# Two of four weight sums made by adding transfers instead of VectorE

## The chip, the cores and the metric

The kernel runs on one core of one Trainium2 chip. The metric is the time of one execution on the device in microseconds (us), lower is better. All arrays are float32. A core has five engines that work side by side, each with its own instructions in a fixed order: TensorE (matrix products; PE in the profile, PEld for its weight loads), VectorE (DVE), ScalarE (ACT), GpSimd (POOL) and SyncE (SP), which here only issues transfers. Transfers between the main memory (HBM) and the on-chip memory (SBUF) run on 16 DMA engines.

## The reference

One layer of a hybrid block works on 256 rows of 4096 numbers. What matters here are its large matrix products; the attention and the convolution between them are left out of this cut:

```python
xn = rms_norm(h, norm_in_g[i])
proj = xn @ w_in[i]                       # q, k, v, z_a, a_c, g_c, z_c: 14336 columns
...
y_a = rms_norm(y_a, attn_out_g[i]) * jax.nn.silu(z_a)
...
y_c = rms_norm(y_c, conv_out_g[i]) * jax.nn.silu(z_c)
h = h + jnp.concatenate([y_a, y_c], axis=-1) @ w_out[i]
gate = jax.nn.sigmoid(rms_norm(h, ple_norm_g[i]) @ w_ple_gate[i] + b_ple_gate[i])
h = h + gate * (p[i] @ w_ple[i])
```

## The kernel before, in words

All large products are made with the 256 rows on the output's partitions (two halves of 128) and 512 columns of the weights at a time. A float32 operand is split into a high and a low part, and one product is three matmuls: high by high, low by high, high by low. For a weight tile the high part is a cast on ScalarE and the low part a subtraction on VectorE (`parts_of`, L191 and L192).

The first 1000 us of the profile use plain products (`product`, L204). After that, the columns z_a and z_c of `w_in`, all of `w_out` and six of the eight column blocks of `w_ple_gate` go through `mixed_product`, two column blocks at a time. It walks over 16 pairs of 128-row blocks of the weights (a pair has 256 rows of K). A plain pair is 2 blocks x 2 column blocks x 2 row halves, eight products, 24 matmuls. A "seven" pair does the same 2 x 2 x 2 block product in Strassen's manner with seven products, P1 to P7, 21 matmuls. It needs sums of weight blocks. With w0 and w1 the pair's two 128-row blocks, each with column halves 0 and 1 of 512:

- ua[0] = w0[0] + w0[1] and ua[1] = w0[1] + w1[1] (L382, L383), used by P5 and P7
- ub[0] = ua[0] + w1[1] and ub[1] = ub[0] + w1[0] (L386, L387), used by P6 and P4

ua and ub are then split like weights (`pair_parts`, into tiles uh and ul). Of w0 only half 0 goes into a product itself (P1); of w1 both halves do (P2, P3).

Which pairs are sevens stands in three lists:

```python
steady = units("1 0* 3 2* 5 4* 7 6* 9 8* 11 10* 13 12* 15 14")
delayed = units("1 3 5 7 0* 9 2* 11 4* 13 6* 15 8* 10 12 14")
late = units("1 3 5 7 9 11 13 15 0* 2 4* 6 8* 10* 12 14")
```

A star marks a seven. There are eleven calls: four for the z columns (one delayed, three steady), four for `w_out` (one late, three steady), three for the gate (one late, two steady). That makes 5 + 21 + 4 + 21 + 4 + 14 = 69 sevens.

Weight tiles come from the pool `wpool`, tag "w", with five buffers of 512 KB, loaded by SyncE (L358). ua and ub share the tag "u" with two buffers, so each waits until the one before the last has been read. The tiles uh and ul have two buffers each as well. The program is written in order of the units; the framework then sets the order on each engine and in each queue by a planner with costs of its own, and puts in the waits. A wait holds up all that stands behind it on the same engine or queue.

Of the kernel before, what the change touches and what calls it, by code (L numbers as in the profile page):

```python
# [13 lines left out]
ALU = mybir.AluOpType  # L14
AX = mybir.AxisListType

P = 128
NB = 512
# [8 lines left out]
def hybrid_block(  # L27
# [23 lines left out]
    nc = tc.nc  # L51
# [117 lines left out]
    def fill(n):  # L169
        for _ in range(min(n, len(later))):  # L170
            later.popleft()()
# [14 lines left out]
    def parts_of(wt, kc, tiles=None):  # L186
        if tiles is None:
            tiles = part_tiles()
        wh, wl = tiles
        made = (  # L190
            nc.scalar.copy(wh[:, :kc, :], wt[:, :kc, :]),  # L191
            nc.vector.tensor_tensor(  # L192
                wl[:, :kc, :], wt[:, :kc, :], wh[:, :kc, :].bitcast(F32), ALU.subtract
            ),
        )
        return (wh, wl), made
# [111 lines left out]
    def pair_parts(src):  # L308

        tiles = [spool.tile([P, 2, NB], F32R, tag=tag, name=tag, bufs=2) for tag in ("uh", "ul")]  # L310
        return parts_of(src, 2, tiles)[0]
# [10 lines left out]
    def mixed_product(w, col, lhs, comb, order, on_helpers, ahead=None, fills=0, on_begin=None):  # L322

        c = [[ps_acc.tile([P, NB], F32, tag="acc", name=f"acc{h}{j}") for j in range(2)] for h in range(NH)]
        helper = {}
        begun, ends = set(), {}
        for n, (_, seven) in enumerate(order):
            for name in ("P1", "P5", "P6", "P7", "P2", "P3", "P4") if seven else ("P2", "P3", "P4", "X"):  # L330
                ends[name] = n
        banks = {"P2": c[0][0], "P3": c[0][1], "P4": c[1][0], "X": c[1][1]}
        made = []

        def add(name, x, w2, n, final):

            for kind, (a, b) in enumerate(((x[0], w2[0]), (x[1], w2[0]), (x[0], w2[1]))):
                made.append(
                    nc.tensor.matmul(  # L339
                        banks[name], a, b, start=name not in begun,  # L340
                        stop=final and ends[name] == n and kind == 2,
                    )
                )
                begun.add(name)

        def block(kb, h):
            t = lhs[kb // 4]
            return [t[:, kb % 4, q, h * P : (h + 1) * P] for q in range(2)]

        last_seven = max(n for n, (_, seven) in enumerate(order) if seven)  # L350
        for n, (pair, seven) in enumerate(order):
            if ahead:
                ahead(pair)
            wts = []
            for k in range(2):
                wt = wpool.tile([P, 2, NB], F32, tag="w", name="wt")
                kb = 2 * pair + k
                nc.sync.dma_start(  # L358
                    wt,
                    w[kb * P : (kb + 1) * P, col : col + 2 * NB].rearrange("q (j n) -> q j n", n=NB),  # L360
                )
                wts.append(wt)
            if not seven:
                for k in range(2):
                    wh, wl = parts_of(wts[k], 2)[0]
                    for j in range(2):
                        for h in range(NH):
                            name = (("P2", "P3"), ("P4", "X"))[h][j]
                            add(name, block(2 * pair + k, h), (wh[:, j], wl[:, j]), n, k == 1)
                fill(fills)  # L370
                continue
            begins = not helper
            if begins:
                for name in ("P1", "P5", "P7", "P6"):
                    helper[name] = ps_tmp.tile([P, NB], F32, tag="tmp", name=f"acc_{name}")
                banks.update(helper)
            w0, w1 = wts
            ua = spool.tile([P, 2, NB], F32, tag="u", name="ua")
            ub = spool.tile([P, 2, NB], F32, tag="u", name="ub")
            plus = partial(nc.vector.tensor_tensor, op=ALU.add)  # L380
            w0h, w0l = parts_of(w0, 1)[0]
            plus(ua[:, 0], w0[:, 0], w0[:, 1])  # L382
            plus(ua[:, 1], w0[:, 1], w1[:, 1])  # L383
            uah, ual = pair_parts(ua)
            w1h, w1l = parts_of(w1, 2)[0]
            plus(ub[:, 0], ua[:, 0], w1[:, 1])  # L386
            plus(ub[:, 1], ub[:, 0], w1[:, 0])  # L387
            ubh, ubl = pair_parts(ub)
            first = len(made)

            def s_of(i):
                t, at = comb[pair // 4], pair % 4
                return [t[:, at + i // 2, q, (i % 2) * P : (i % 2 + 1) * P] for q in range(2)]

            k0, k1 = 2 * pair, 2 * pair + 1
            add("P1", block(k0, 0), (w0h[:, 0], w0l[:, 0]), n, True)
            add("P5", s_of(1), (uah[:, 0], ual[:, 0]), n, True)
            add("P7", s_of(0), (uah[:, 1], ual[:, 1]), n, True)
            add("P2", block(k1, 0), (w1h[:, 0], w1l[:, 0]), n, True)
            add("P3", s_of(3), (w1h[:, 1], w1l[:, 1]), n, True)  # L400
            add("P6", s_of(2), (ubh[:, 0], ubl[:, 0]), n, True)
            add("P4", block(k1, 1), (ubh[:, 1], ubl[:, 1]), n, True)
            if begins and on_begin:
                on_begin()
            if begins:
                tc.add_manual_dep(
                    made[first].ins, last_transpose[0].ins.name,
                    mybir.DependencyInfo(mybir.DependencyClass.NoSync, mybir.DependencyReason.DATA),
                    reason="transposes before the helpers take their banks",
                )  # L410
            if n == last_seven:
                on_helpers(helper)
            fill(fills)
        return c
# [383 lines left out]
    def gated(ys, c0, col, r_y, order):  # L798

        z = sum_tiles()  # L800

        def on_helpers(helper):
            nc.scalar.copy(z[0][:, 0], helper["P1"])
            helper_sums(helper, z)

        acc = mixed_product(w_in0, col + c0 * NB, xT, xS, order, on_helpers, fills=2)
        for h, j in ((0, 0), (1, 0), (0, 1), (1, 1)):
            zz, y = z[h][:, j], ys[c0 + j][:, h, :]
            tt(zz, acc[h][j], zz, ALU.subtract if j else ALU.add)  # L809
            nc.scalar.activation(zz, zz, AF.Silu, scale=r_x[:, h : h + 1])  # L810
            later.append(partial(stt, y, y, r_y[:, h : h + 1], zz, ALU.mult, ALU.mult))
# [17 lines left out]
    for c0 in range(0, D // NB, 2):  # L829
        for j in range(2):  # L830
            hc = act.tile([P, NH, NB], F32, tag="act", name="hc")
            c = c0 + j
            nc.sync.dma_start(
                hc, x[0, :, c * NB : (c + 1) * NB].rearrange("(h q) n -> q h n", q=P)
            )
            hs.append(hc)

        def on_helpers(helper):
            z = sum_tiles()
            h00, h01, h10, h11 = (hs[c0 + j][:, h, :] for h in range(NH) for j in range(2))  # L840
            tt(h00, helper["P1"], h00, ALU.add)
            helper_sums(helper, z)
            tt(h01, h01, z[0][:, 1], ALU.subtract)
            tt(h10, h10, z[1][:, 0], ALU.add)
            tt(h11, h11, z[1][:, 1], ALU.subtract)

        acc = mixed_product(
            w_out[0], c0 * NB, yT, yS, steady if c0 else late, on_helpers,
            ahead=None if c0 else y_ahead, fills=2,
        )  # L850
        for h, j in ((0, 0), (1, 0), (0, 1), (1, 1)):
            hc = hs[c0 + j][:, h, :]
            tt(hc, acc[h][j], hc, ALU.add)
            later.append(partial(square_sum, ssq_h[:, h, c0 + j : c0 + j + 1], hc))
# [48 lines left out]
    def gated_pair(c0, order, ahead):  # L903
# [7 lines left out]
        def on_helpers(helper):  # L911
# [8 lines left out]
            fgs.extend(broadcast_row(final_g, (c0 + j) * NB, NB) for j in range(2))  # L920

        acc = mixed_product(
            w_ple_gate[0], c0 * NB, hT, hS, order, on_helpers, ahead=ahead, fills=4,
            on_begin=on_begin,
# [71 lines left out]
```

## Time and profile before

| | |
|---|---|
| median of 3 runs | 2078.56 us (2078.46 to 2079.0) |
| profiled execution | 2077.91 us |
| its span, first to last instruction | 2075.9 us |
| mean granted TensorE clock | 0.997 |
| read from HBM | 406.39 MB |

The profile page gives, for one execution, the busy time of each engine, the chain of work that ended last, and groups of instructions by line. A group's row has the line, the engine and operation, output and inputs with their shapes, the count, then the busy time in us with the mean duration of one in ns, then how long the engine was idle just before such instructions and what ended most of that. In a row of a timeline the first number is the start in us and the second the duration. In a row of the busy time by stages stand the stretch, its length, then the busy time of TensorE, its weight loads, VectorE, ScalarE and GpSimd with their counts of instructions, the granted TensorE clock, the busy share of the DMA engines and GB/s. In a row of waits stand who waited, for whom, the total in us, how often, and the longest.

### The profile page before, as it was taken

To read this page: it belongs to the slowest core of one execution; us is meant where nothing else is said; L and a number is where in the kernel's file an instruction comes from. 1 tells how busy PE (TensorE), PEld (TensorE's weight loads), DVE (VectorE), ACT (ScalarE), POOL (GpSimd) and SP (SyncE) were. 2 spreads that over 40 slices of the span, in tenths; PEclk is the share of its full clock that TensorE was granted. 3 is DMA by queue.
4 is the path that set the end of the run, shared out by engine and by line. 5 is a ranking of instruction groups with operands and counts; after the bars stand their busy time and mean duration, and the time that the engine had idled before them with its cause. 6 is when DMAs were issued, how large, how long until landed. Compare 5 with 4: busy or idle time off the path is not lost.

```text
span 2075.9 us, 25611 instructions
## 1 busy us (share of the span) xinstructions
PE 2053.2 (99%) x9242; PEld 1691.1 (81%) x9242; DVE 1638.5 (79%) x2246; ACT 1087.0 (52%) x1385; POOL 39.8 (2%) x38
## 2 busy tenths in 40 slices
PE   9999999999999999999999999999999999999997
PEld 7888888888888888888888888878888878888886
DVE  5599965498547955765889889899898989999954
ACT  7444345444444435564556555575555656656543
POOL 0000000000000002200000000000000000000000
PEclk9999999999999999999999999999999999999999
DMA  8666665666566665655666666665666556666664
GB/s 291 190 185 192 190 192 176 193 190 186 182 191 186 191 193 175 184 180 197 195 206 194 201 201 203 214 227 200 202 203 205 201 182 202 210 227 213 218 210 165
DMA packets 170329, 412.27 MB, mean 199 GB/s; under 512 B 13006, under 2 KB 16222, under 8 KB 170202
## 3 DMA queue, kind: packets, MB, share of 16 engines
q1 hardware_dynamic: 169914, 410.11, 62.0%
q8 instruction: 72, 1.18, 0.2%
q10 hardware_dynamic: 288, 0.52, 0.1%
q14 instruction: 55, 0.45, 0.1%
HBM read 406.39 MB, written 4.19 MB: 198 GB/s over the span
## 4 chain that ended last, share of the span: by engine, by line
PE 95%; DVE 2%; DMA 1%; issue 1%; ACT 1%; POOL 0%; SPq 0%; ACTq 0%; POOLq 0%; DVEq 0%
PE acc L204 50%; PE acc L339 33%; PE acc_P L339 9%; DVE wl L192 1%; PE tmp_ps L150 1%; DMA wt<-in_w_in_dram 0%; PE tmp_ps L672 0%; PE tmp_ps L687 0%; PE tmp_ps L705 0%; DMA xin<-in_x_dram 0%; DMA wt<-in_w_out_dram 0%; ACT wh L191 0%; DVE z L809 0%; PE tmp_ps L711 0%; PE tmp_ps L712 0%
## 5 line engine op out<-in xcount | busy, mean ns | idle before, releaser
L191 ACT CAST wh<-wt 128x1024 fp32r<-128x1024 f32 (+1 forms) x741 | 742.9, 1011 | 751.6 <-PE acc L204 499.4
L192 DVE TENSOR_TENSOR wl<-wt,wh 128x1024 fp32r<-128x1024 f32 (+1 forms) x741 | 871.0, 1184 | 303.5 <-ACT wh L191 297.4
L204 PE MATMUL acc<-wh,big_t 128*128 128x512 f32 x3040 | 951.0, 392 | 0.6 <-ACT big_t L136 0.3
L204 PEld LDWEIGHTS acc<-wh,big_t 128*128 128x128 f32 x3040 | 569.9, 188 | 117.0 <-ACT big_t L136 1.0
L339 PE MATMUL acc<-wh,big_t 128*128 128x512 f32 x1972 | 610.3, 391 | 4.4 <-ACT big_t L136 3.5
L204 PE MATMUL acc<-wl,big_t 128*128 128x512 f32 x1520 | 593.0, 390 | 0.1
L339 PEld LDWEIGHTS acc<-wh,big_t 128*128 128x128 f32 x1972 | 369.6, 188 | 82.3 <-ACT big_t L136 4.0
L339 PE MATMUL acc<-wl,big_t 128*128 128x512 f32 x986 | 384.5, 391 | 1.0 <-DVE wl L192 0.6
L204 PEld LDWEIGHTS acc<-wl,big_t 128*128 128x128 f32 x1520 | 285.8, 188 | 58.4 <-DVE wl L192 0.5
L339 PEld LDWEIGHTS acc<-wl,big_t 128*128 128x128 f32 x986 | 185.7, 188 | 42.4 <-DVE wl L192 3.7
L523 DVE SCALAR_TENSOR_TENSOR cv<-uT,dw,cv 128x256 f32<-128x256 f32 x480 | 202.7, 483 | 0.5
L191 ACT CAST uh<-ub 128x1024 fp32r<-128x1024 f32 x69 | 72.6, 1052 | 84.8 <-DVE ub L387 68.1
L339 PE MATMUL acc_P<-uh,big_t 128*128 128x512 f32 x366 | 112.1, 389 | 0.0
L191 ACT CAST uh<-ua 128x1024 fp32r<-128x1024 f32 x69 | 72.7, 1054 | 45.1 <-DVE ua L383 43.7
L192 DVE TENSOR_TENSOR ul<-ub,uh 128x1024 fp32r<-128x1024 f32 x69 | 84.2, 1221 | 14.9 <-ACT uh L191 14.6
L192 DVE TENSOR_TENSOR ul<-ua,uh 128x1024 fp32r<-128x1024 f32 x69 | 84.1, 1219 | 0.0
L339 PEld LDWEIGHTS acc_P<-uh,big_t 128*128 128x128 f32 x366 | 68.6, 188 | 14.3
L382 DVE TENSOR_TENSOR ua<-wt 128x512 f32<-128x512 f32 x69 | 47.5, 689 | 40.7 <-DMA wt<-in_w_in_dram 18.6
L339 PE MATMUL acc_P<-ul,big_t 128*128 128x512 f32 x183 | 70.8, 391 | 0.0
L383 DVE TENSOR_TENSOR ua<-wt 128x512 f32<-128x512 f32 x69 | 47.3, 685 | 1.9 <-DMA wt<-in_w_in_dram 1.7
L387 DVE TENSOR_TENSOR ub<-ub,wt 128x512 f32<-128x512 f32 x69 | 47.5, 688 | 1.3
L386 DVE TENSOR_TENSOR ub<-ua,wt 128x512 f32<-128x512 f32 x69 | 47.2, 685 | 0.0
(193 smaller groups left out, 1114.4 us busy)
## 6 DMA issues: line engine op xcount, KB each, us to landing
wt<-in_w_in_dram SPq DMA_DIRECT2D x447, 512.0 KB, 3.8
wt<-in_w_out_dram SPq DMA_DIRECT2D x128, 512.0 KB, 4.3
wt<-in_w_ple_gate_dram SPq DMA_DIRECT2D x128, 512.0 KB, 4.2
wt<-in_w_pw_dram SPq DMA_DIRECT2D x32, 512.0 KB, 4.4
hc<-in_x_dram SPq DMA_DIRECT2D x8, 512.0 KB, 4.5
wt<-in_w_ple_dram SPq DMA_DIRECT2D x8, 512.0 KB, 4.3
out_dram<-hc SPq DMA_DIRECT2D x16, 256.0 KB, 2.9
xin<-in_x_dram SPq DMA_DIRECT2D x7, 512.0 KB, 8.5
```

What stands on the lines that cost most here:

```text
L150: nc.tensor.transpose(pt[:, i * T + h * P : i * T + (h + 1) * P], src[:, h, b * P : (b + 1) * P], ident,)
L191: nc.scalar.copy(wh[:, :kc, :], wt[:, :kc, :]),
L192: nc.vector.tensor_tensor(wl[:, :kc, :], wt[:, :kc, :], wh[:, :kc, :].bitcast(F32), ALU.subtract),
L204: nc.tensor.matmul(acc, a, b[:, k, :], start=kb == 0 and kind == 0, stop=kb == kblocks - 1 and kind == 2,)
L339: nc.tensor.matmul(banks[name], a, b, start=name not in begun, stop=final and ends[name] == n and kind == 2,)
L382: plus(ua[:, 0], w0[:, 0], w0[:, 1])
L383: plus(ua[:, 1], w0[:, 1], w1[:, 1])
L386: plus(ub[:, 0], ua[:, 0], w1[:, 1])
L387: plus(ub[:, 1], ub[:, 0], w1[:, 0])
L523: nc.vector.scalar_tensor_tensor(cv[:, i, :], uT[:, i, k : k + T], dw[:, b, k : k + 1], cv[:, i, :], ALU.mult, ALU.add,)
```

## The change

In a seven pair only the half of w0 that is used by itself is loaded into its weight tile. SyncE loads both halves of w0 into ua (`ua[0] = w0[0]`, `ua[1] = w0[1]`), and GpSimd then issues a transfer that reads `w0[1]` and `w1[1]` from HBM and adds them onto ua's two halves as it writes. The two VectorE adds that made ua are gone; those that make ub stay. w0's half and w1 are loaded as before, so `w0[1]` and `w1[1]` are read twice or more from HBM.

```diff
             for k in range(2):
                 wt = wpool.tile([P, 2, NB], F32, tag="w", name="wt")
                 kb = 2 * pair + k
+                n_j = 1 if seven and k == 0 else 2
                 nc.sync.dma_start(
-                    wt,
-                    w[kb * P : (kb + 1) * P, col : col + 2 * NB].rearrange("q (j n) -> q j n", n=NB),
+                    wt[:, :n_j],
+                    w[kb * P : (kb + 1) * P, col : col + n_j * NB].rearrange("q (j n) -> q j n", n=NB),
                 )
                 wts.append(wt)
...
             w0h, w0l = parts_of(w0, 1)[0]
-            plus(ua[:, 0], w0[:, 0], w0[:, 1])
-            plus(ua[:, 1], w0[:, 1], w1[:, 1])
+            k = 2 * pair
+            nc.sync.dma_start(
+                ua, w[k * P : (k + 1) * P, col : col + 2 * NB].rearrange("q (j n) -> q j n", n=NB)
+            )
+            nc.gpsimd.dma_start(
+                ua,
+                w[k * P : (k + 2) * P, col + NB : col + 2 * NB].rearrange("(j q) n -> q j n", q=P),
+                accum_op=ALU.add,
+            )
             uah, ual = pair_parts(ua)
```

## The prediction

> **What bounds the kernel now.** I read the head of the page first, then the chain of work that ended last.
>
> ```profile
> span 2075.9 us, 25611 instructions
> PE 2053.2 (99%) x9242; PEld 1691.1 (81%) x9242; DVE 1638.5 (79%) x2246; ACT 1087.0 (52%) x1385; POOL 39.8 (2%) x38
> ...
> PE 95%; DVE 2%; DMA 1%; issue 1%; ACT 1%; POOL 0%; SPq 0%; ACTq 0%; POOLq 0%; DVEq 0%
> PE acc L204 50%; PE acc L339 33%; PE acc_P L339 9%; DVE wl L192 1%; PE tmp_ps L150 1%; DMA wt<-in_w_in_dram 0%; PE tmp_ps L672 0%; PE tmp_ps L687 0%; PE tmp_ps L705 0%; DMA xin<-in_x_dram 0%; DMA wt<-in_w_out_dram 0%; ACT wh L191 0%; DVE z
> ```
>
> TensorE is busy for 99% of the span and carries 95% of the chain; the products that the change touches (L339) are 42% of it. VectorE carries 2%. So work taken from VectorE shortens the kernel only where TensorE now waits for VectorE. Those waits are listed in the view of waits of the weight loads, and the stage's totals stand in the busy time by stages:
>
> ```profile
> PEld acc L339 <- DVE wl L192: 3.7, 7, 1.1
> PEld acc_P L339 <- DVE ul L192: 1.0, 5, 0.3
> ...
> 1000.00:1980.00 980.00, 974.54 (x4342) 803.34 (x4341) 886.22 (x1128) 575.45 (x712) 3.70 (x2) 1.00 0.62 206
> ```
>
> From 1000 to 1980 us, where all the seven-product units lie, TensorE is idle for 980 - 974.5 = 5.5 us, and 4.7 us are all that its weight loads wait for VectorE's remainders there. VectorE is 886 / 980 = 90% busy, the DMA engines 62%, GpSimd hardly at all. The most that a relieved VectorE can give is thus about 5 us, a quarter of a per cent. The question is what the new transfers delay.
>
> **What the change removes.** The two adds per unit, from the page's groups:
>
> ```profile
> L191 ACT CAST uh<-ua 128x1024 fp32r<-128x1024 f32 x69 | 72.7, 1054 | 45.1 <-DVE ua L383 43.7
> L192 DVE TENSOR_TENSOR ul<-ua,uh 128x1024 fp32r<-128x1024 f32 x69 | 84.1, 1219 | 0.0
> L382 DVE TENSOR_TENSOR ua<-wt 128x512 f32<-128x512 f32 x69 | 47.5, 689 | 40.7 <-DMA wt<-in_w_in_dram 18.6
> L383 DVE TENSOR_TENSOR ua<-wt 128x512 f32<-128x512 f32 x69 | 47.3, 685 | 1.9 <-DMA wt<-in_w_in_dram 1.7
> ```
>
> 47.5 + 47.3 = 94.8 us of VectorE over 69 units, 1.4 us a unit. By the waits above that is worth 0 to 5 us; I book nothing, because the wait below takes its place.
>
> **What it adds.** Per unit SyncE loads half of w0 (256 KB), all of w1 (512 KB), and now ua itself (512 KB); GpSimd then issues a transfer of 512 KB that adds onto ua. That is 768 KB a unit more from HBM, 69 x 0.786 MB = 54 MB on the 206 GB/s x 980 us = 202 MB of the stage: the DMA share goes from 0.62 towards 0.62 x 1.27 = 0.79 if the time stayed. No bound by itself.
>
> The cost is order. The sum in ua now exists only after two transfers, one after the other: the plain load into ua may start only when the previous unit's readers have left that buffer, and the adding transfer only when the load has landed. In the timeline of VectorE, four units of one product, the previous unit's readers and the next unit's adds stand like this:
>
> ```profile
> 1505.25 0.69 DVE L383 TENSOR_TENSOR ua<-wt 128x512 f32<-128x512 f32 x1
> ...
> 1509.45 1.22 DVE L192 TENSOR_TENSOR ul<-ua,uh 128x1024 fp32r<-128x1024 f32 x1
> ...
> 1526.27 0.69 DVE L383 TENSOR_TENSOR ua<-wt 128x512 f32<-128x512 f32 x1
> ...
> 1539.73 0.68 DVE L383 TENSOR_TENSOR ua<-wt 128x512 f32<-128x512 f32 x1
> ...
> 1556.34 0.69 DVE L383 TENSOR_TENSOR ua<-wt 128x512 f32<-128x512 f32 x1
> ...
> 1559.81 1.22 DVE L192 TENSOR_TENSOR ul<-ua,uh 128x1024 fp32r<-128x1024 f32 x1
> ...
> 1564.75 0.69 DVE L382 TENSOR_TENSOR ua<-wt 128x512 f32<-128x512 f32 x1
> ...
> 1566.49 0.69 DVE L383 TENSOR_TENSOR ua<-wt 128x512 f32<-128x512 f32 x1
> ```
>
> Two things are read here. From ua complete (1556.34 + 0.69 = 1557.03) to its last reader's end (1559.81 + 1.22 = 1561.03) pass 4.0 us; in the unit before the product's end 4.7 (1505.94 to 1510.67). And within a product ua is due every 1566.49 - 1556.34 = 10.15 us, which is TensorE's own pace: 21 matmuls of the seven products and 24 of the plain unit between. At a product's border the distance is 21.0 (1505.25 to 1526.27) and then 13.5 us (to 1539.73). The pool "u" has two buffers for ua and ub in turn, so ua of the next unit gets the buffer that ua of this one leaves.
>
> One round of ua after the change is therefore: load + adding transfer + readers. The rows for the first two terms (line view of L358, and the page's DMA issues):
>
> ```profile
> DMA to landing us min/median/max: 3.2/4.2/6.7
> ...
> hc<-in_x_dram SPq DMA_DIRECT2D x8, 512.0 KB, 4.5
> ...
> xin<-in_x_dram SPq DMA_DIRECT2D x7, 512.0 KB, 8.5
> ```
>
> Load of 512 KB: 4.2 us, the median of the same size from the same queue (bounds 3.2 and 6.7). Readers: the cast 1.05 and the remainder 1.22 with nothing between make 2.3 us, the trace shows up to 4.7; I take 3.5, since VectorE has less to do but its order still puts other remainders between. The adding transfer is in no row. The page's DMA queues, with the loads of SyncE (q1), those of ACT at the start (q10) and code, have none of GpSimd's:
>
> ```profile
> q1 hardware_dynamic: 169914, 410.11, 62.0%
> q8 instruction: 72, 1.18, 0.2%
> q10 hardware_dynamic: 288, 0.52, 0.1%
> q14 instruction: 55, 0.45, 0.1%
> ```
>
> It moves as much as a plain 512 KB load, so 3.2 us is its floor; it also reads ua back before it writes it, so a second plain load's time, 2 x 4.2 = 8.4 us, near the slowest 512 KB row (8.5), is the upper bound. I take the middle, 6.3 us, as neither row is nearer in kind. Round: 4.2 + 6.3 + 3.5 = 14.0 us against 10.15. Bounds: 3.2 + 3.2 + 2.3 = 8.7 and 6.7 + 8.5 + 4.7 = 19.9.
>
> The Trainium skill (Collectives: The Full Stack, on why ReduceScatter has half of AllGather's rate) says that the add in a DMA costs no time of its own but needs two source reads on one ring; with DMA: Bandwidth & Descriptors, section Anatomy of one DMA, which gives 2.0 us plus bytes by 436 GB/s, that makes an estimated 2.0 + 2 x 1.2 = 4.4 us here. The same formula for a plain load gives 3.2 us, which is the trace's minimum and not its median of 4.2. No run here shows an adding transfer yet; by 4.4 the sum would be that of the second rival below.
>
> **What is queued behind the new waits.** On SyncE the load into ua waits for the buffer, and the weight loads of the next units (L358) behind it; five "w" buffers cover that while the round is under the 10 us of two units. On ACT the cast of ua, behind it those of w1 and of the plain unit; on VectorE the remainder of ua, behind it ub's two adds; on TensorE the products P5 and P7, behind them the whole plain unit. GpSimd's queue holds nothing else of weight in the stage (3.70 us in 2 instructions), so passing its queue costs nothing; the smaller load of w0 gains nothing either, since P5 and P7 follow P1 at once.
>
> **The sum.** A steady product has seven such units in 21.0 + 13.5 + 5 x 10.15, about 82.5 to 85 us; I use 82.5, the shorter, as the rounds follow 1505.25 at that pace. Seven rounds of 14.0 are 98.0, 15.5 us more, if the chain of rounds runs on through the border; if the border gives it nothing, six rounds cost 3.85 each, 23.1. I take 19. There are eight steady products, six of this kind and two for the gate, which carry extra products of w_ple and so have some 4 us more cover each: 6 x 19 + 2 x 15 = 144. The "delayed" product has five units with four gaps of one pair, 4 x 3.85 = 15 at most, I take 11. The two "late" ones have three gaps, of which the last has no plain unit between (21 of 45 matmuls, 21/45 x 10.15 = 4.7 us, so 9.3 are missing): 2 x 3.85 + 9.3 = 17, less 4 of lead at the border, 13 each. Together 144 + 11 + 26 = 181 us. The profiled execution took 2077.9 us (span 2075.9 and 2.0 around it), the median of the runs shown is 2078.6, so the profile stands for it: 2078 + 181 = 2259 us.
>
> TensorE's clock falls when it waits. In the busy time by stages, one window has it:
>
> ```profile
> 1346.00:1366.00 20.00, 17.86 (x84) 14.46 (x83) 16.64 (x32) 13.61 (x24) 0.00 (x0) 0.91 0.60 200
> ```
>
> 2.1 us of idle time, then a granted clock of 0.91 over 20 us, that is 1.8 us lost. If each new wait cost that, TensorE would need 10.15 + 1.8 = 12.0 us a pair, still under the 14.0 of the round: it is covered while the round is longer than 12 us, and I book nothing. The Trainium skill (TensorE: Matmul & The Clock Gate, Part 1) warns against idle gaps over about 3.4 us, for they halve the clock until the array has been busy as long again; the waits of some 3.9 us forecast here are of that size, and an estimated 1.7 us would go at each. The trace agrees on the fall (0.91 over 20 us), and shows it after less idle time. Where the loss is not covered it is the fourth rival.
>
> **The rivals.** *First: the round is hidden.* If the adding transfer lands in the floor of 3.2 us and the readers need 2.3, the round is 4.2 + 3.2 + 2.3 = 9.7 us, under 10.15, and TensorE never waits for ua. VectorE's 94.8 us are then free and at most 5 us of waits go: 2073 to 2078 us, the end on the other side. It decides below a round of 10.15 us. For it: HBM and the DMA engines have room (0.62). Against it: it needs the floor in one transfer and in the readers together, every time, with 27% more traffic.
>
> *Second: the add costs little.* With 4.3 us for it, a plain load's 4.2 and hardly more, the round is 12.0: seven rounds are 84 against 82.5 (1.5 to 11.1 us a product, I take 6), for the gate 3, the delayed one 4, the late ones 7: 36 + 6 + 4 + 14 = 60 us, 2138 us. Here the clock's loss is not covered, so it would rather be above that.
>
> *Third: the adding transfer takes 8.4 us or more.* Round 16.1, seven are 112.7: 30 to 36 a product, I take 33; gate 28; delayed 20; late 20: 198 + 56 + 20 + 40 = 314 us, 2392 us. For it: HBM read, read-back and write share engines that are 62% busy.
>
> *Fourth: the clock's loss comes on top.* A slower TensorE reads ua's two parts later, and the cast of the next ua needs the buffers of those parts (tag "uh", two for ua and ub in turn); if that ends last, each of the 58 waits (8 x 6 + 4 + 2 x 3) costs its 1.8 us too: 104 us more, 2363 us. For it: the window at 1346. Against it: there are 14.0 us a round and TensorE needs 12.0 of them.
>
> *Fifth: the change doesn't do what it says*, for instance because the load into ua is started much earlier than the buffers allow by my reading: then nothing waits, as in the first.
>
> **How the numbers follow.** Forecast (add 5.3 to 8 us) 0.45, centre 2259; second rival 0.21; third 0.21; fourth 0.04; first and fifth together 0.09. About 0.2% is what a measurement of this kernel can tell from no change, 4 us. The first and fifth split into 0.04 faster and 0.05 the same; all others are slower, 0.91. The range takes in the second rival down to a round of 11.3 (2110 us, 32 us over before) the fourth, and the third up to a round of 17 (seven are 119, 372 us over, 2450 us); beyond it lie about 0.1 below and 0.1 above.
>
> **What would show it.** In the changed kernel's page: a DMA queue of GpSimd with 69 issues of 512 KB and its time to landing (6.3 forecast); the groups L382 and L383 gone; the cast of ua idle before it for several us, put down to the adding transfer, 69 times; TensorE busy some 90% instead of 99%, its waits before P5; ua's casts 14 us apart inside a product; a DMA share about 0.7 in the stage; SyncE waiting for the remainder of ua. I am wrong if the casts of ua stay 10.15 us apart, or if TensorE waits somewhere else, for plain weights behind SyncE's wait above all.

## The result, and the profile after

The changed kernel takes 2466.1 us (median of 4 runs, 2464.9 to 2470.1) against 2078.8 us: a ratio of 1.187, 95% interval 1.186 to 1.189, 387 us more. The direction and the mechanism were forecast; the size was 207 us short and lies 16 us above the range.

The page of the changed kernel, its head, its DMA queues, two groups and the DMA issues:

```profile
span 2468.3 us, 25824 instructions
PE 2215.4 (90%) x9242; PEld 1758.5 (71%) x9242; DVE 1558.3 (63%) x2108; ACT 1073.9 (44%) x1385; POOL 124.1 (5%) x107
...
q1 hardware_dynamic: 179850, 428.20, 56.3%
q0 software_dynamic: 18768, 36.18, 8.7%
...
L191 ACT CAST uh<-ua 128x1024 fp32r<-128x1024 f32 x69 | 72.2, 1046 | 557.5 <-DMA ua<-in_w_out_dram 216.7
L394 DVE TENSOR_TENSOR ub<-ua,wt 128x512 f32<-128x512 f32 x69 | 47.6, 690 | 348.9 <-issue 199.5
...
ua<-in_w_in_dram SPq DMA_DIRECT2D x26, 512.0 KB, 4.0
ua<-in_w_in_dram POOLq DMA_DIRECT2D x26, 512.0 KB, 8.5
ua<-in_w_out_dram SPq DMA_DIRECT2D x25, 512.0 KB, 4.2
ua<-in_w_out_dram POOLq DMA_DIRECT2D x25, 512.0 KB, 8.9
```

TensorE fell from 99% to 90% busy. VectorE did lose 80 us of work (1638.5 to 1558.3), and the kernel is slower all the same. There is a new queue, q0, GpSimd's. ScalarE now stands idle for 557.5 us before its 69 casts of ua, 45.1 us before; the cast waits for the adding transfer. The last rows give the price: 8.5 to 8.9 us to landing, where the plain load ahead of it takes 4.0 to 4.2. From HBM 54 MB more are read (460.65 against 406.39 MB): in each seven unit both halves of w0 and the second half of w1 are read twice.

The busy time by stages, in the columns shown before, for the stretch that was 980 us long:

```profile
1000.00:2367.00 1367.00, 1133.92 (x4341) 868.71 (x4340) 804.92 (x991) 561.01 (x711) 86.54 (x70) 0.89 0.66 186
```

980 us have become 1367: all 387 us are here. TensorE is idle for 233 us in it (5.5 before) and busy for 159 us more with the same matmuls, at a granted clock of 0.89. Whether that slower clock is a cause or only fills waiting time is asked below. The DMA share is 0.66 (0.62 before), at 186 GB/s (206 before): on the average over the stage, the DMA engines have hardly more to do.

One round of ua can be followed from engine to engine. These are rows of the timelines of ScalarE, VectorE, SyncE, GpSimd and again ScalarE (start, duration, what, and in brackets the idle time before and what ended it):

```profile
1895.09 1.04 ACT L191 CAST uh<-ua 128x1024 fp32r<-128x1024 f32 x1 [9.52 <-DMA ua<-in_w_out_dram]
...
1896.43 1.22 DVE L192 TENSOR_TENSOR ul<-ua,uh 128x1024 fp32r<-128x1024 f32 x1
...
1897.68 0.33 SPq L384 DMA_DIRECT2D ua<-in_w_out_dram  x1
1898.28 4.87 SPq L359 DMA_DIRECT2D wt<-in_w_out_dram  x4
...
1902.28 1.21 POOL L387 DMA_DIRECT2D ua<-in_w_out_dram  x1 [14.69 <-DVE wl L192]
...
1910.39 1.05 ACT L191 CAST uh<-ua 128x1024 fp32r<-128x1024 f32 x1 [9.90 <-DMA ua<-in_w_out_dram]
```

The last reader of ua ends at 1896.43 + 1.22 = 1897.65. The load is issued 0.03 us later, GpSimd issues the adding transfer 4.60 us after that, and the next cast starts 8.11 us after this issue. From cast to cast 15.3 us. Nothing in this chain waits for TensorE. The bracket on GpSimd's row names VectorE; as that remainder had long been done, the wait is really for the load. The second SyncE row matters too: right behind ua's load SyncE sends the weight loads that had waited behind it, and they share the DMA engines with the adding transfer.

The busy time by stages for three stretches of this round, from the load's issue to GpSimd's, from there to the next cast, and from the cast to the next load's issue:

```profile
1897.68:1902.28 4.60, 3.97 (x9) 3.18 (x10) 4.60 (x5) 2.81 (x3) 0.01 (x1) 0.50 0.79 253
1902.28:1910.39 8.11, 8.11 (x34) 6.61 (x33) 0.51 (x1) 0.00 (x0) 1.21 (x1) 0.89 0.84 214
1910.39:1912.72 2.33, 1.31 (x5) 0.47 (x3) 1.94 (x3) 1.57 (x2) 0.00 (x0) 1.00 0.00 0
```

The DMA share is 0.79 and 0.84 while the two transfers run and 0.00 while ua is read. Over the 69 units the medians are 0.73, 0.84 and 0.03. The stage's 0.66 is an average over these.

TensorE's waits in the stage mostly end with a cast by ScalarE. The two largest rows of its view of waits, 1000 to 2367 us:

```profile
PE acc_P L339 <- ACT wh L191: 79.5, 30, 4.3
PE acc_P L339 <- ACT uh L191: 42.7, 12, 7.1
```

The larger row is a cast of weights. In the round above, the cast of w0's half, for P1, stands on ScalarE right behind the cast of ua that waits (1896.04 behind 1895.09), so TensorE stops ahead of P1 already, and not only ahead of P5.

Over the 69 units the medians are: release to issue 0.03 us, load 4.0, landing to GpSimd's issue 0.68 (for these two, over the 61 units for which the trace tells the load's landing), adding transfer 8.6, landing to the end of the last reader 3.1. That sums to 16.4; of the 68 distances between landings, the 53 inside products (under 19 us) have a median of 16.2.

### The profile page after: what moved, and what is told of

It reads as the page before. It is cut to its first block, busy times and chain, and to the rows that moved or that the text cites. A ratio compares the mean times of both kernels' runs of the same rounds, so it can differ in the third digit from the quotient of the medians.

```text
span 2468.3 us, 25824 instructions
## 1 busy us (share of the span) xinstructions
PE 2215.4 (90%) x9242; PEld 1758.5 (71%) x9242; DVE 1558.3 (63%) x2108; ACT 1073.9 (44%) x1385; POOL 124.1 (5%) x107
## 3 DMA queue, kind: packets, MB, share of 16 engines
q0 software_dynamic: 18768, 36.18, 8.7%
HBM read 460.65 MB, written 4.19 MB: 188 GB/s over the span
## 5 line engine op out<-in xcount | busy, mean ns | idle before, releaser
L204 PE MATMUL acc<-wh,big_t 128*128 128x512 f32 x3040 | 953.0, 393 | 2.1 <-ACT wh L191 2.1
L339 PE MATMUL acc<-wh,big_t 128*128 128x512 f32 x1972 | 649.9, 412 | 39.5 <-ACT wh L191 28.9
L204 PEld LDWEIGHTS acc<-wh,big_t 128*128 128x128 f32 x3040 | 571.2, 189 | 119.0 <-ACT wh L191 2.5
L204 PE MATMUL acc<-wl,big_t 128*128 128x512 f32 x1520 | 594.4, 391 | 0.9 <-DVE wl L192 0.9
L339 PEld LDWEIGHTS acc<-wh,big_t 128*128 128x128 f32 x1972 | 393.0, 201 | 136.0 <-ACT wh L191 40.6
L339 PE MATMUL acc<-wl,big_t 128*128 128x512 f32 x986 | 407.5, 413 | 27.3 <-DVE wl L192 27.1
L204 PEld LDWEIGHTS acc<-wl,big_t 128*128 128x128 f32 x1520 | 286.6, 189 | 59.5 <-DVE wl L192 1.7
L191 ACT CAST uh<-ua 128x1024 fp32r<-128x1024 f32 x69 | 72.2, 1046 | 557.5 <-DMA ua<-in_w_out_dram 216.7
L339 PEld LDWEIGHTS acc<-wl,big_t 128*128 128x128 f32 x986 | 195.6, 198 | 90.6 <-DVE wl L192 50.2
L339 PE MATMUL acc_P<-uh,big_t 128*128 128x512 f32 x366 | 144.4, 484 | 42.7 <-ACT uh L191 42.7
L339 PEld LDWEIGHTS acc_P<-uh,big_t 128*128 128x128 f32 x366 | 87.2, 242 | 65.4 <-ACT uh L191 47.7
L339 PE MATMUL acc_P<-wh,big_t 128*128 128x512 f32 x138 | 50.8, 452 | 79.5 <-ACT wh L191 79.5
L339 PE MATMUL acc_P<-ul,big_t 128*128 128x512 f32 x183 | 90.6, 497 | 9.6 <-DVE ul L192 9.5
L339 PEld LDWEIGHTS acc_P<-wh,big_t 128*128 128x128 f32 x138 | 25.2, 202 | 95.2 <-ACT wh L191 92.2
L339 PE MATMUL acc_P<-wl,big_t 128*128 128x512 f32 x69 | 37.9, 549 | 34.1 <-DVE wl L192 33.6
```

What stands on the lines that cost most here:

```text
L204: nc.tensor.matmul(acc, a, b[:, k, :], start=kb == 0 and kind == 0, stop=kb == kblocks - 1 and kind == 2,)
L339: nc.tensor.matmul(banks[name], a, b, start=name not in begun, stop=final and ends[name] == n and kind == 2,)
```

## The experiments

The kernel before ran beside each of them on the same chip; the ratios are to it.

**What the adding transfer's time is made of.** In the first, the transfer doesn't add:

```diff
             nc.gpsimd.dma_start(
                 ua,
                 w[k * P : (k + 2) * P, col + NB : col + 2 * NB].rearrange("(j q) n -> q j n", q=P),
-                accum_op=ALU.add,
             )
```

> The adding transfer becomes a plain one of the same bytes from the same queue (ua then holds w0[1] and w1[1] instead of the sums, so the products are not the reference's). Theory A, a round of ua (load, issue on GpSimd, adding transfer, readers) sets the pace, and the adding itself is what makes the transfer long: landing falls from 8.6 us to about 5, the round from 16.4 to about 12.8 us, the time to 2078 + 56 x 2.6 + 2 x 8.1 = about 2240 us. Rival B, the transfer is long because GpSimd issues it: landing stays near 8.6 us and the time near 2466 us.

2319.8 us in this run (e1), ratio 1.116 (1.113 to 1.119). The line view of the issuing line:

```profile
DMA to landing us min/median/max: 4.1/6.7/8.6
```

and the page's queue row:

```profile
q0 software_dynamic: 9936, 36.18, 4.6%
```

A plain transfer of the same bytes from GpSimd takes 6.7 us, 8.6 with the add. So theory and rival each had a part: 242 of the 387 us stay without any adding. The queue's row gives the DMA engines' own share: 4.6% of 2324.6 us over 69 transfers is 1.55 us each, against 8.7% of 2468.3 us, 3.11 us, with the add. Adding doubles the engines' time for the same bytes. It also doubles the packets, as the two rows of q0 show: 18768 with the add, 9936 without. In the packets of the two traces, the first moves 3.1 us after GpSimd's issue with the add and 2.4 us without, and from the first to the last pass 5.0 and 3.7 us (medians).

Next, the same plain transfer issued by SyncE (`nc.sync.dma_start` in place of `nc.gpsimd.dma_start`, without the add):

> The second transfer onto ua is plain and issued by SyncE instead of GpSimd (ua holds w0[1] and w1[1] instead of the sums, so the products are not the reference's). Theory A: the second transfer lands in about 4.3 us instead of the 6.7 of the plain one from GpSimd and without its 0.7 us of issue, but SyncE now waits for the first load with all weight loads behind it. If the round alone counts: 4.2 + 0.1 + 4.3 + 3.1 = 11.7 us, 2078 + 56 x 1.5 + 2 x 7 = about 2176 us. Rival E, the long landing comes from sharing the DMA engines with the weight loads and not from who issues it: landing near 6.5 us, 2290 to 2320 us.

2168.0 us in this run (e5), ratio 1.043 (1.042 to 1.045), near theory A's 2176. But the second transfer lands in

```profile
DMA to landing us min/median/max: 3.8/5.4/6.8
```

5.4 us, not 4.3: it is still slower than the first load, so not all of what I put down to GpSimd is GpSimd's. From GpSimd it takes 1.3 us more, although less moves beside it there (SyncE's queue moved 1188 KB meanwhile in e1, here 1484 KB, medians), and 0.68 us pass between the first load's landing and GpSimd's issue.

Half the bytes by the adding transfer:

```diff
             nc.gpsimd.dma_start(
-                ua,
-                w[k * P : (k + 2) * P, col + NB : col + 2 * NB].rearrange("(j q) n -> q j n", q=P),
+                ua[:, 0],
+                w[k * P : (k + 1) * P, col + NB : col + 2 * NB],
                 accum_op=ALU.add,
             )
+            plus(ua[:, 1], ua[:, 1], w1[:, 1])
```

> Only ua[0] is made by the adding transfer (256 KB), ua[1] by VectorE onto the loaded half. Theory A with a price that grows with the bytes: about 6 us to landing, a round of 13.9 us, 2078 + 56 x 3.7 + 2 x 9.2 = about 2305 us. If the transfer's price is a fixed start and not its bytes: landing 8.6 us, near 2466 us.

2295.8 us in this run (e3), ratio 1.105 (1.104 to 1.107), 9 us from theory A's number. The landing:

```profile
DMA to landing us min/median/max: 4.1/5.8/7.7
```

It is 5.8 us, so half of the bytes save 2.8 us of 8.6.

Then the transfers beside it. In the changed kernel, the time to landing of the 69 adding transfers grows with what SyncE's queue moves meanwhile: a straight line through them (correlation 0.77) gives 5.1 us alone and 2.9 us for each 1000 KB; the median unit has 1264 KB beside it, two and a half weight loads. To test it, fewer weights are loaded:

```diff
             for k in range(2):
+                if k and not seven:
+                    wts.append(wts[0])
+                    continue
                 wt = wpool.tile([P, 2, NB], F32, tag="w", name="wt")
```

> The change, but a plain pair loads only its first 512 KB of weights and uses them for its second block too (half of the plain pairs' weights are left out; every cast, remainder and matmul stays). If the adding transfer is long because it shares the DMA engines with the weight loads (over the 69 units of the change its time to landing fits 5.1 us plus 2.9 us per 1000 KB that SyncE's queue moves meanwhile, median 1264 KB), it lands in about 6.9 us, the round is 14.7 us, the time 2078 + 56 x 4.5 + 2 x 10 = about 2350 us. If its length is its own, it stays at 8.6 us and the time near 2466 us.

2368.1 us in this run (e11), ratio 1.141 (1.139 to 1.143). The bytes beside it fell to a median of 668 KB and the landing to

```profile
DMA to landing us min/median/max: 5.7/7.5/10.5
```

7.5 us (6.9 expected). So fewer bytes beside the adding transfer do make it land earlier, by 1.1 us for about half of them. The line itself proves less than it seems to: a transfer that takes longer for any reason has more moved beside it. Counted only over the first 5.5 us after the issue, which every one of the 69 takes, the bytes beside it and its time have a correlation of 0.29 in the changed kernel. Other runs with the same adding transfer don't lie on one line either: 552 KB beside it and 7.0 us in e4 below, 780 KB and 6.2 us in e8, 1812 KB and 8.9 us in e6 (medians). How much of the 8.6 us is sharing stays open; its direction is shown.

**The load alone.** VectorE adds onto the loaded ua; w0 is loaded whole and GpSimd transfers nothing:

```diff
-                n_j = 1 if seven and k == 0 else 2
+                n_j = 2
...
-            nc.gpsimd.dma_start(
-                ua,
-                ...
-            )
+            plus(ua[:, 0], ua[:, 0], w0[:, 1])
+            plus(ua[:, 1], ua[:, 1], w1[:, 1])
```

> ua is still loaded by SyncE, but VectorE adds w0[1] and w1[1] onto it in place, from fully loaded w0 and w1; no transfer of GpSimd. Theory A: the round is load 4.0 + adds 1.4 to 3 + readers 3, about 8.4 to 10 us, under the 10.2 us of TensorE: 2078 to 2110 us. Rival D, SyncE's wait for ua's buffer holds up the weight loads behind it, or the added traffic does it: then a good part of the 387 us stays, over 2200 us.

2091.8 us in this run (e2), ratio 1.007 (1.005 to 1.008). The load with its wait for the buffer, all that is queued behind it on SyncE and two thirds of the added traffic cost 14 us together. The rest, over 370 us, comes with the second transfer of the chain. Rival D falls.

**The clock.** Sixteen matmuls with a zero operand (`zero_op`, a tile of zeros made at the start) stand ahead of the wait in 58 units:

```diff
+            for i in range(0 if begins else 16):
+                nc.tensor.matmul(banks["P1"][:64], zero_op[0], w0h[:, 0], start=False, stop=False)
             add("P1", block(k0, 0), (w0h[:, 0], w0l[:, 0]), n, True)
```

> 16 more matmuls per seven unit with a zero stationary operand, added onto P1 (58 units; the sums do not change), 3.6 us of TensorE work placed ahead of the waits. Theory A: TensorE then needs 13.8 us a pair, still under the round of 16.4: the time stays within 1% of 2466 us, and the granted clock rises from 0.89 in the stage. Rival C, the clock's fall costs time of its own (58 x 1.8 us): the time falls by up to 100 us to about 2365 us. If TensorE sets the pace after all: up by about 58 x 3.6 = 209 us.

2488.3 us in this run (e4), ratio 1.198 (1.195 to 1.200), 0.9% over the changed kernel. By stages:

```profile
1000.00:2367.00 1367.00, 1234.34 (x5191) 935.82 (x5190) 786.48 (x971) 563.71 (x697) 86.54 (x70) 0.96 0.65 184
```

The granted clock rose from 0.89 to 0.96 and TensorE did some 850 more matmuls in the same stretch, and no time was won. The parts of the round were others here, adding transfer 7.0 us and readers 4.8, and that they came to nearly the same round (16.5 us between landings inside products, 16.2 in the changed kernel) is in part chance. What the run shows is that TensorE had room for 3.6 us more work in a round and that a higher clock brought nothing by itself. So the 159 us of slower matmuls in the changed kernel are most likely waiting time filled.

**The buffer.** If the chain of rounds through one buffer is the cause, a second buffer for ua takes it away. SBUF had no room, so ub was made in place in w1's tile and both "u" buffers went to ua; the control is the kernel before with the same move:

```diff
-            ub = spool.tile([P, 2, NB], F32, tag="u", name="ub")
...
-            plus(ub[:, 0], ua[:, 0], w1[:, 1])
-            plus(ub[:, 1], ub[:, 0], w1[:, 0])
-            ubh, ubl = pair_parts(ub)
+            plus(w1[:, 1], ua[:, 0], w1[:, 1])
+            plus(w1[:, 0], w1[:, 1], w1[:, 0])
+            ubh, ubl = pair_parts(w1)
...   (P6 and P4 take the other halves of ubh and ubl)
```

> The change with ub made in place in w1's tile, so that both buffers of tag u are ua's; all results the same. Theory A: two rounds overlap, so a ua is due every 16.4 / 2 = 8.2 us, under TensorE's 10.2: nearly all of the 387 us goes, 2078 to 2110 us (the pair of sevens without a plain unit between may cost some us). Rival E, shared DMA engines or GpSimd's queue are the bound and not the buffer: over 2250 us.

> The kernel before with the same move of ub into w1's tile, as a control for e6: VectorE makes both sums. All theories: within 0.5% of the kernel before, 2068 to 2089 us. If VectorE's relief by the transfers is worth anything, e6 is below this one; by the waits of the kernel before at most 5 us.

With the transfers (e6) 2105.7 us, ratio 1.014 (1.013 to 1.016); without them (e7, the control) 2116.5 us, 1.019 (1.017 to 1.020). From the page with the transfers:

```profile
ua<-in_w_in_dram POOLq DMA_DIRECT2D x26, 512.0 KB, 8.9
...
ua<-in_w_out_dram POOLq DMA_DIRECT2D x25, 512.0 KB, 9.0
```

358 of the 387 us went, with the adding transfer as slow as ever (8.6 to 9.0 us for the three weight arrays). What is left needs no transfers to explain it: the control has it too, and more. I had expected the control within 0.5%; holding w1 longer costs 1.9%. Beside this control the transfers win about 11 us.

That pointed to a version that might beat both kernels, with buffers of ua's own:

```diff
-            ua = spool.tile([P, 2, NB], F32, tag="u", name="ua")
-            ub = spool.tile([P, 2, NB], F32, tag="u", name="ub")
+            ua = spool.tile([P, 2, NB], F32, tag="ua", name="ua", bufs=2)
+            ub = spool.tile([P, 2, NB], F32, tag="u", name="ub", bufs=1)
...
-        junk = spool.tile([P, NB], mybir.dt.bfloat16, tag="junk", name="junk")
+        junk = spool.tile([P, NB], mybir.dt.bfloat16, tag="junk", name="junk", bufs=1)
...   (tag "row": bufs=3 -> 2; tag "ln_stat": cpool -> spool)
```

> The change with two buffers of ua's own and one of ub's; the 4 KB a partition come from a third buffer of the rows (tag row), a second of the scratch of the square sums (junk), and the layer norm's two statistics, which move to the first stage's scratch. ub is made as in the change. Theory A: no round waits for ua's buffer, so 2078 to 2090 us, and if VectorE's relief counts (e6 was 11 us under its control e7) about 2068 to 2076 us. Rival E, the transfers of GpSimd and their traffic cost by themselves: 2095 us or more.

> Control: the kernel before with the same buffers taken away and nothing given to ua. All theories: 2076 to 2085 us.

> Control: the kernel before with e8's buffers, two for ua and one for ub, both sums by VectorE. Theory A: TensorE was 99% busy before, so 2072 to 2085 us; what e8 is under this one is the worth of taking the two adds from VectorE.

The two controls are where they should be: 2079.7 us, ratio 1.001 (1.000 to 1.002), for e9, and 2081.8 us, 1.002 (1.001 to 1.003), for e10. The changed kernel with these buffers (e8) takes 2145.8 us, 1.033 (1.032 to 1.035): 318 of the 387 us gone, but no gain, and theory A's 2078 to 2090 is missed by 56 us. The view of waits of VectorE, 1000 to 2000 us, and that of TensorE show where it waits now:

```profile
DVE ub L394 <- DMA wt<-in_w_in_dram: 59.8, 18, 5.3
DVE wl L192 <- ACT wh L191: 46.6, 42, 2.5
DVE ub L394 <- DMA wt<-in_w_out_dram: 44.2, 14, 4.4
DVE ul L192 <- ACT uh L191: 27.0, 17, 8.1
DVE ub L394 <- DMA wt<-in_w_ple_gate_dram: 25.0, 9, 4.9
...
PE acc L339 <- DVE wl L192: 31.6, 30, 2.5
```

ua is hardly late any more: ScalarE stands idle for 34 us in all before its casts, 557.5 in the changed kernel. VectorE stands at ub's first add until w1 lands (129 us in all), and the remainders of the plain unit, for which TensorE waits, stand behind it. I tried to have w1 land sooner, by loading it ahead of w0 in a seven unit:

> e8 with w1 loaded ahead of w0 in the seven units. In e8 VectorE idles 129 us in all at ub's first add until w1 has landed, with the plain unit's remainders queued behind it. If that is what keeps e8 69 us over the kernel before, the time falls to about 2090 us or below. If the added traffic is, it stays near 2146 us.

2202.2 us in this run (e12), ratio 1.062 (1.059 to 1.064): worse by 56 us. The order of the two loads is not the cure: the wait at ub's first add grew (174 us in all), and the adding transfer now took 9.2 to 10.0 us to landing, 6.1 to 7.7 in e8. Whether w1 is late because of the traffic or because of the order that the planner chose for the queues was not settled. No version ran below the kernel before.

## Why the prediction was wrong in size

**The bound, the removed work.** The prediction booked nothing for it, and in the changed kernel the round covers whatever it is worth. Only e6 beside its control shows something of it, 11 us, and that control itself runs 40 us over the kernel before. So the bound of 5 us, read from TensorE's waits, was not tested for the kernel as it was.

**The chain of the round.** Right, link by link: load after the previous readers, adding transfer after the load, readers after that, and a round longer than TensorE's pair of units. The two-buffer runs (e6 with its control, and e8 with its controls) are the proof, since they leave every transfer in place and take the chaining away.

**The term that failed: the adding transfer.** I put it at 6.3 us, midway between a plain load's floor and two plain loads. It takes 8.6 us to landing and 0.68 us more before its issue, 9.3 in all; load (4.0 against 4.2) and readers (3.1 against 3.5) were close. What I called the upper bound, 8.4 to 8.5 us, is what the median just passed; the slowest of the 69 took 10.7. What I left out is shown in the runs: the transfer is issued by GpSimd (1.3 us more than from SyncE for a plain one), whose queue I had put at no cost, and 1264 KB of weight loads run beside it, as SyncE's queue lets go of them just when ua's load is issued. I treated the DMA share of 0.62 as room left over, an average over the stage; but while this transfer was under way the engines were 84% busy, its own packets included.

The Trainium skill (Collectives: The Full Stack, the section on ReduceScatter against AllGather) has the add cost a second read on the same ring and no more. The trace agrees on a doubling (3.11 us of engine time against 1.55, in twice as many packets); that a second read makes it, no run here shows. The estimate of 4.4 us to landing drawn from it was half the measured 8.6, and under the fastest of the 69 (5.9).

**The second step that failed: the border between products.** I gave each product back 4 us or more of lead at its border. With a round of 16.4 us and nothing given back, the sum of the prediction reads 56 gaps x (16.4 - 10.2) + 2 x (16.4 - 4.7) = 371 us; measured are 387. So the border gives nothing and takes a little. Of the 207 us that the forecast was short, a round of 16.4 in place of 14.0 makes 137 by this sum, the credit at the borders 53, and some 16 are left over. VectorE's timeline at a border shows why there is no credit:

```profile
1853.20 1.23 DVE L192 TENSOR_TENSOR ul<-ua,uh 128x1024 fp32r<-128x1024 f32 x1 [8.36 <-ACT uh L191]
1854.34 0.68 DVE L791 TENSOR_TENSOR z<-acc_P,z 128x512 f32<-128x512 f32 x1
...
1862.07 0.68 DVE L394 TENSOR_TENSOR ub<-ua,wt 128x512 f32<-128x512 f32 x1
```

The ua that landed at 1852 is split at once, but its last reader, ub's first add, stands in VectorE's queue behind the sums of the helpers and comes 10 us later. The buffer is free only then, and the lead is gone. The prediction counted only the cast and the remainder as readers; but ub's first add reads ua too. In the first unit of every one of the eleven products it is the last reader. In the eight steady ones it ends 7.1 to 17.9 us after ua has landed, against the median of 3.1.

**The rivals.** The third had the price of the transfer (8.4 us or more) and with the same false credit 2392 us; with none it would have come to 2430. The fourth, the clock's loss on top, found no support in e4. Of the signs I named, most came: q0 with 69 transfers, L382 and L383 gone, TensorE at 90%, a DMA share of 0.66, ScalarE idle before the casts of ua. Others came differently: 61 of the 69 casts waited for the adding transfer, TensorE waited more for weight casts behind them than for ua's own, and ua landed every 16.2 us inside a product, not every 14.

The Trainium skill (TensorE: Matmul & The Clock Gate, Part 1) foretells the fall of the clock for gaps over about 3.4 us. The trace shows the fall (0.89 in the stage), but after shorter gaps too: only 15 of TensorE's 141 gaps over 0.3 us in the stage were longer than 3.4 us, and in the round shown above two gaps of 1.0 and 0.6 us (1911 to 1913 us) were followed by 6.8 us at half the clock. That the fall cost no time here rests on e4 alone.

## What to carry to other kernels

A transfer that adds onto a buffer needs the buffer free, loaded and then added to, all in series: price the whole round from one release to the next, and compare it with the pace at which the buffer is due, not with the work taken from an engine. If the round is longer, count the buffers first; a second one gave back over 80% here, while the engine time saved showed as 11 us at most, beside a control that was itself slower. List every reader of the buffer, and look at where each stands in its engine's queue at a border between products. Price a new transfer at the DMA traffic of its own moment, which the waits just before it set, and not at the stage's mean share.

## What the runs showed of the hardware

- An adding transfer of 512 KB onto SBUF kept each DMA engine busy for about 3.1 us, a plain one of the same bytes from the same queue for 1.55 us.
- To landing it took 5.9 us at best and 8.6 us in the median, with 1264 KB of weight loads moved meanwhile; 7.5 us with 668 KB (e11). The plain transfer from GpSimd took 6.7 us (e1), from SyncE 5.4 us (e5).
- In this stage the granted clock of TensorE fell to half for 3.4 or 6.8 us at a time, after idle gaps that were mostly shorter than 3.4 us (median 1.0 us).
- From the landing of a load to GpSimd's start of a transfer that waited for it, 0.68 us passed in nearly every unit (0.63 to 0.88 us); SyncE's issue followed a release after 0.03 us.
